# A hybrid encoder block on one core: the opening stage written in program order

## The chip, the cores and the metric

The kernel runs on one core of one Trainium2 chip. The core has TensorE (PE, matrix products; PEld is its weight load), VectorE (DVE), ScalarE (ACT), GpSimd (POOL) and SyncE (SP, which issues DMA transfers here). Each engine works through its own list of instructions in order, and waits where one needs a result of another engine. The metric is the device time of one execution in microseconds (us). Before the change: 984.22 us, the median of three runs (984.08 to 984.52).

## The reference

One layer of an encoder trunk on x of 512 positions by 1024 channels, float32. What matters for the opening:

```python
def rms_norm(x, g):
    xf = x.astype(jnp.float32)
    y = xf * lax.rsqrt(jnp.mean(xf * xf, axis=-1, keepdims=True) + EPS)
    return (y * g.astype(jnp.float32)).astype(x.dtype)
...
        hn = rms_norm(h, g_mix_pre[i])
        proj = hn @ w_in[i]
        z_sgu, z_conv, z_pool, z_gate = jnp.split(proj, SPLITS, axis=-1)
...
    a, gate = jnp.split(z, 2, axis=-1)
    h = a * jax.nn.sigmoid(gate)
```

Behind that come three token mixers (a spatial gating unit, a depthwise convolution of width 31, and multi-scale pooling), their merging by gates, an output product, a SwiGLU layer and a gated embedding. The change touches none of these.

## The kernel before

Channels lie on the 128 partitions, positions along the free axis. x is eight tiles of 128 channels by 512 positions (x_all), and k counts them. Every float32 operand of a product is split in two parts: a rounded high part made on ScalarE (a CAST, or an ACTIVATE where a gain is multiplied in) and the low remainder made on VectorE. A product is then three: high by high, high by low, low by high (mm3, L207).

The opening computes the first three pairs of convolution blocks before the norm of x is known. For that, x times the gain g_mix_pre is split into xg (split_scaled, L349), and the weight slice k of 768 columns (first_raw, loaded by L134) into first (split, L356). The slices 5 to 7 are loaded into the buffers named raw. For each k, 18 products go into six PSUM banks, ps_first (L414). The inverse norm comes out later as a factor: the squares of x are made on ScalarE and added up in x_sums, by GpSimd from the third on (L358). One product with a constant matrix makes the mean (ps_stat), and rsqrt makes x_inv in eight dependent steps on VectorE (inv_rms, in the loop over k at STAT_K = 4). Then each tile of x is multiplied by gain and x_inv (tile nrm), and split into hn. The products behind the opening, ps_ag, take hn and the weight blocks of in_w_mix: five more pairs, of 24 products for a block. A block is loaded into a raw buffer (three of them), and split into hi and lo.

What sets the order: the kernel is written against a framework that schedules instructions itself, from buffers and dependencies. Only inside a block `with order():` do the instructions issued through dve, act_e and pe keep the written order among themselves (InOrder, L55). The opening before stands outside such a block, so the scheduler is free there. The loads go through SyncE in the written order: x_all and the weight slice in turn for each k. A transfer waits in that queue until one of eight earlier ones has landed.

Of the kernel before, what the change touches and what calls it, by code (L numbers as in the profile page):

```python
# [12 lines left out]
AF = mybir.ActivationFunctionType  # L13
ALU = mybir.AluOpType
PSUM = bass.MemoryType.PSUM

P = 128
T = 512
H = 256
D = 1024  # L20
KT = D // P
# [16 lines left out]
N_VEC = len(VECS) * KT  # L38
# [5 lines left out]
N_WARM = 8  # L44
# [1 line left out]
TAPS = (4, 3, 5, 3, 5)  # L46
TAPS_U = 4

STAT_K, STAT_A, STAT_H, STAT_F = 4, 2, 7, 2
MIX_CUT = ((), (0,), (1, 2), (3, 4, 5, 6, 7))  # L50
PLE_CUT = (1, 2, 3, 4, 5, 6, 8)
PLE_SPLIT = 3
# [29 lines left out]
def hybrid_block(  # L82
# [7 lines left out]
    nc = tc.nc  # L90
    order = InOrder(tc)
    dve, act_e, pe = order.engine(nc.vector), order.engine(nc.scalar), order.engine(nc.tensor)
# [9 lines left out]
    def bank(name):  # L102
        return psum.tile([P, T], F32, tag="ps", name=name)

    def wide_tile(name):
        return wide.tile([P, KT, T], F32, tag="wide", name=name)

    def slot(tag, name, dt=F32R, shape=(2, T)):
        return act.tile([P, *shape], dt, tag=tag, name=name, bufs=6 if tag == "tm" else 8)

    def t2(name, n=T):
        return tmp.tile([P, n], F32, tag="t2", name=name)

    def row(name):
        return stat.tile([P, T], F32, tag="row", name=name)


    vec = const.tile([P, N_VEC + WIDTH * KT], F32, name="vec")
    x_all = wide_tile("x_all")
    first_all = wide.tile([P, KT * T], F32, tag="wide", name="first_all")  # L120
    first_raw = []

    def first_cuts(k):
        return ((0, 2 * P), (2 * P, N_FIRST)) if k == 0 else ((0, N_FIRST),)

    nc.scalar.dma_start(out=vec[:, :N_VEC], in_=vecs[:, :N_VEC])
    for k in range(KT):
        if k < 5:
            first_raw.append(first_all[:, k * N_FIRST:(k + 1) * N_FIRST])
        else:  # L130
            first_raw.append(stream.tile([P, D], F32, tag="raw", name="raw")[:, :N_FIRST])
        nc.sync.dma_start(out=x_all[:, k], in_=xT[:, k])
        for c0, c1 in first_cuts(k):
            nc.sync.dma_start(out=first_raw[k][:, c0:c1], in_=w_first[k][:, c0:c1])  # L134

    def col(name, k):
        i = VECS.index(name) * KT + k
        return vec[:, i:i + 1]
# [9 lines left out]
    warm_up = const.tile([P, T], BF16, name="warm_up")  # L148
    dve.memset(warm_up, 0.0)
    ps = psum.tile([P, T], F32, tag="pst", name="ps_warm", bufs=1)  # L150
    for _ in range(N_WARM):
        pe.matmul(ps, lhsT=warm_up[:, :P], rhs=warm_up, start=True, stop=True)
    ident = const.tile([P, P], F32, name="ident")
    make_identity(nc, ident)
    cnt_i = const.tile([P, WINDOWS[-1]], I32, name="cnt_i")
# [6 lines left out]
    def split(hi, lo, src):  # L162
        act_e.copy(hi, src)
        dve.tensor_tensor(out=lo, in0=src, in1=hi, op=ALU.subtract)

    def split_scaled(hi, lo, src, scale):

        act_e.activation(out=hi, in_=src, func=AF.Copy, scale=scale)
        dve.scalar_tensor_tensor(out=lo, in0=src, scalar=scale, in1=hi,
                                       op0=ALU.mult, op1=ALU.subtract)  # L170
# [34 lines left out]
    weights = Weights()  # L205
# [6 lines left out]
    def blk(w, k):  # L212
        return w[:, k * P:(k + 1) * P]
# [23 lines left out]
    def rsqrt(y, a, t):  # L237

        dve.tensor_scalar(out=y.bitcast(I32), in0=a.bitcast(I32), scalar1=-0.5,
                          scalar2=RSQRT_SEED, op0=ALU.mult, op1=ALU.add)  # L240
        dve.tensor_tensor(out=t, in0=y, in1=y, op=ALU.mult)
        dve.scalar_tensor_tensor(out=t, in0=t, scalar=-RSQRT_C2 * RSQRT_S, in1=a,
                                 op0=ALU.mult, op1=ALU.mult)
        dve.scalar_tensor_tensor(out=y, in0=t, scalar=RSQRT_C1 * RSQRT_S, in1=y,
                                 op0=ALU.add, op1=ALU.mult)
        dve.tensor_tensor(out=t, in0=y, in1=y, op=ALU.mult)
        dve.tensor_tensor(out=t, in0=t, in1=a, op=ALU.mult)
        dve.scalar_tensor_tensor(out=t, in0=t, scalar=-10.0 / 3.0 * RSQRT_S ** 2, in1=t,
                                 op0=ALU.add, op1=ALU.mult)
        dve.scalar_tensor_tensor(out=y, in0=t, scalar=5.0 * RSQRT_S ** 4, in1=y,  # L250
                                 op0=ALU.add, op1=ALU.mult)

    def channel_mean(sums):

        ps = psum.tile([P, T], F32, tag="pst", name="ps_stat", bufs=1)
        ps = ps[:, :sums.shape[1]]
        pe.matmul(ps, lhsT=mean_mat, rhs=sums, start=True, stop=True)
        return ps

    def inv_rms(sums, y):  # L260

        rsqrt(y, channel_mean(sums), t2("rs_t", sums.shape[1]))

    def square(src, name="sq"):
        sq = t2(name, src.shape[1])
        act_e.activation(out=sq, in_=src, func=AF.Square)
        return sq

    def add_square(sums, src, i, engine):

        if i == 0:
            act_e.activation(out=sums, in_=src, func=AF.Square)
        else:
            add_sq(sums, square(src), i, engine)

    def add_sq(sums, sq, i, engine):
        if i == 1:
            dve.scalar_tensor_tensor(out=sums, in0=sq, scalar=EPS * D / P, in1=sums,
                                     op0=ALU.add, op1=ALU.add)
        else:  # L280
            engine.tensor_tensor(out=sums, in0=sums, in1=sq, op=ALU.add)
# [63 lines left out]
    xg = [slot("br", f"xg{k}") for k in range(KT)]  # L345
    x_sums = row("x_sums")
    first = []
    for k in range(KT):
        split_scaled(xg[k][:, 0], xg[k][:, 1], x_all[:, k], col("g_mix_pre", k))  # L349
        if k < 7:  # L350
            pair = [slot("cv" if k < 4 else "tm", "first", shape=(D,)) for _ in range(2)]
        else:
            pair = [stream.tile([P, D], F32R, tag=t, name=t) for t in ("hi", "lo")]
        first.append([w[:, :N_FIRST] for w in pair])
        for c0, c1 in first_cuts(k):
            split(first[k][0][:, c0:c1], first[k][1][:, c0:c1], first_raw[k][:, c0:c1])  # L356
    for k in range(KT):
        add_square(x_sums, x_all[:, k], k, nc.gpsimd)  # L358
    weights.ahead(2)
    nc.sync.dma_start(out=vec[:, N_VEC:], in_=vecs[:, N_VEC:])  # L360


    h_conv = [slot("cv", f"h_conv{i}", F32) for i in range(4)]
# [29 lines left out]
    def glu(k, ps_a, ps_g, scale=None):  # L393
        sig = t2("sig")
        src = ps_g
        if scale is not None:
            dve.tensor_tensor(out=sig, in0=ps_g, in1=scale, op=ALU.mult)
            src = sig
        act_e.activation(out=sig, in_=src, func=AF.Sigmoid)
        if scale is not None:  # L400
            dve.tensor_tensor(out=sig, in0=sig, in1=scale, op=ALU.mult)
        dve.tensor_tensor(out=h_of(k), in0=ps_a, in1=sig, op=ALU.mult)
        queue_conv(k)

    hn = [slot("hn", f"hn{k}") for k in range(KT)]
    x_inv = row("x_inv")
    conv_sum = row("conv_sum")
    banks = [bank("ps_first") for _ in range(2 * N_RAW)]
    for k in range(KT):
        if k == STAT_K:  # L410
            inv_rms(x_sums, x_inv)
        for i, (w, a) in enumerate(((0, 0), (1, 0), (0, 1))):
            for j, ps in enumerate(banks):
                pe.matmul(ps, lhsT=blk(first[k][w], j), rhs=xg[k][:, a],  # L414
                                 start=k == 0 and i == 0, stop=k == KT - 1 and i == 2)
    for i in range(KT):
        t = t2("nrm")
        dve.scalar_tensor_tensor(out=t, in0=x_all[:, i], scalar=col("g_mix_pre", i),
                                       in1=x_inv, op0=ALU.mult, op1=ALU.mult)
        split(hn[i][:, 0], hn[i][:, 1], t)  # L420
    for k in range(N_RAW):
        glu(k, banks[2 * k], banks[2 * k + 1], x_inv)
    for k in range(N_RAW, KT):
        pair = []
        for _ in range(2):
            ps = bank("ps_ag")
# [119 lines left out]
    def branch_tile(acts, taps):  # L546
        ps = bank("ps_br")
        product(ps, weights.get(), acts)
        drain(taps)
        return ps  # L550

    for n in range(KT + SGU_LAG):
# [7 lines left out]
        else:  # L560
            i = n - SGU_LAG
            ps = branch_tile(sgu_T, TAPS[2])
# [49 lines left out]
    for n in range(KT + POOL_LAG):  # L612
# [39 lines left out]
    for n in range(KT):  # L652
        ps = branch_tile(conv_T, 0)
# [64 lines left out]
    with order():  # L718
# [25 lines left out]
        banks = [bank("ps_f") for _ in range(2 * N_PAIR)]  # L744
# [65 lines left out]
    for n in range(KT - 2):  # L810
        ps = bank("ps_fo")
# [25 lines left out]
    with order():  # L837
        ps = bank("ps_fo")
        halves = [bank("ps_fo") for _ in HALVES]
        ffn_out(ps, KT - 2, 0, weights.get(2))  # L840
        w = weights.get(1)
        for b, hs in zip(halves, HALVES):
            ffn_out(b, KT - 1, 0, w, hs)
        w = weights.get(1)
        ffn_out(ps, KT - 2, 1, w)
        weights.ahead(3)
        w = weights.get(2)
# [9 lines left out]
        c0, c1 = ffn_out_cuts[1]  # L857
# [10 lines left out]
        k = 0  # L868
# [9 lines left out]
        banks = [bank("ps_pg") for _ in range(N_LAST)]  # L878
# [82 lines left out]
```

## Time and profile before

| what | value |
|---|---|
| median of three runs | 984.22 us |
| the profiled execution | 983.63 us |
| its span, first to last instruction | 981.9 us |
| TensorE busy | 973.8 us (99%) |
| VectorE busy | 677.3 us (69%) |
| ScalarE busy | 346.1 us (35%) |
| GpSimd busy | 88.2 us (9%) |
| granted clock | 1.0 |

The time is some 1.7 us longer than the span, by what lies around the first and last instruction. The busy share of TensorE counts products as modelled; a product at half its clock also counts as busy. So the share says that TensorE seldom waits, and nothing of how fast its products follow each other. The granted clock is that of a limiter and reads 1.00 even where the products are at the lower of the two clock levels; that level shows in the distance of their starts.

### The profile page before, as it was taken

How to read it: one execution, taken by the hardware profiler on the slowest of the kernel's cores; microseconds unless marked ns; L12 is line 12 of the kernel's file. 1: busy time of each engine (PE TensorE's matmuls, PEld its weight loads, DVE VectorE, ACT ScalarE, POOL GpSimd, SP SyncE). 2: the span in 40 equal slices, each digit the busy share in tenths (PEclk: the TensorE clock that was granted, in tenths of full speed). 3: DMA queues.
4: the chain of work that ended last, by engine and by line, in shares of the span. 5: the costliest groups of instructions: out<-in, count | busy, mean ns of one | idle time of the engine just before them, and what ended most of it. 6: DMA issues, size and time to landing. Idle time of an engine off the chain costs nothing.

```text
span 981.9 us, 11718 instructions
## 1 busy us (share of the span) xinstructions
PE 973.8 (99%) x4682; PEld 819.2 (83%) x4682; DVE 677.3 (69%) x903; ACT 346.1 (35%) x483; POOL 88.2 (9%) x64
## 2 busy tenths in 40 slices
PE   9999999999999999999999999999999999999998
PEld 6788888788888878888888998888888888888897
DVE  7898789999988899957555787544444432223575
ACT  6422333332224332146435443323232322223442
POOL 4000004000013712160000010000000000000000
PEclk9999999999999999999999999999999999999999
DMA  6433331323322322332338112323322333334312
GB/s 233 137 108 107 109 106 65 107 69 104 107 81 81 101 103 86 105 110 68 126 96 272 62 38 74 104 90 104 98 96 93 98 91 104 92 92 139 109 43 86
DMA packets 30006, 100.53 MB, mean 102 GB/s; under 512 B 3456, under 2 KB 3968, under 8 KB 29952
## 3 DMA queue, kind: packets, MB, share of 16 engines
q1 hardware_dynamic: 29808, 99.75, 30.9%
q8 instruction: 36, 0.59, 0.2%
q14 instruction: 18, 0.15, 0.0%
q10 hardware_dynamic: 144, 0.04, 0.0%
HBM read 97.68 MB, written 2.10 MB: 102 GB/s over the span
## 4 chain that ended last, share of the span: by engine, by line
PE 88%; DVE 7%; issue 2%; DMA 1%; ACT 1%; SPq 0%; DVEq 0%; ACTq 0%
PE ps_f L69 25%; PE ps_br L69 13%; PE ps_fo L69 12%; PE ps_gate L69 12%; PE ps_ag L69 5%; PE ps_pg L69 5%; PE ps_o L69 5%; PE ps_z L69 4%; PE ps_nat L69 4%; DVE lo L69 2%; DVE acc L69 2%; PE ps_ple L69 1%; PE ps_pool L69 1%; DVE v_all L69 1%; DMA first_all<-in_w_first 1%
## 5 line engine op out<-in xcount | busy, mean ns | idle before, releaser
L69 ACT CAST hi<-raw 128x1024 fp32r<-128x1024 f32 (+3 forms) x158 | 162.5, 1030 | 456.3 <-PE ps_br L69 88.4
L69 DVE TENSOR_TENSOR lo<-raw,hi 128x1024 fp32r<-128x1024 f32 (+3 forms) x158 | 206.2, 1306 | 107.0 <-ACT hi L69 106.5
L69 DVE SCALAR_TENSOR_TENSOR acc<-h_conv,vec,acc 128x511 f32<-128x511 f32 (+14 forms) x240 | 183.3, 764 | 5.2
L69 PE MATMUL ps_f<-hg,hi 128*128 128x512 f32 (+1 forms) x624 | 184.5, 379 | 0.0
L69 PEld LDWEIGHTS ps_f<-hg,hi 128*128 128x128 f32 x624 | 115.1, 188 | 21.7
L69 PE MATMUL ps_gate<-hn,hi 128*128 128x512 f32 x384 | 119.6, 392 | 0.9 <-DVE gated L69 0.9
L69 PE MATMUL ps_f<-hg,lo 128*128 128x512 f32 (+1 forms) x312 | 118.0, 379 | 0.0
L69 PE MATMUL ps_fo<-f,hi 128*128 128x512 f32 (+1 forms) x396 | 111.0, 366 | 0.0
L69 PEld LDWEIGHTS ps_gate<-hn,hi 128*128 128x128 f32 x384 | 72.0, 188 | 17.1 <-DVE gated L69 1.3
L69 PEld LDWEIGHTS ps_fo<-f,hi 128*128 128x128 f32 x396 | 71.7, 189 | 12.2
L69 PE MATMUL ps_nat<-hi,hn 128*128 128x512 f32 x256 | 78.8, 390 | 0.0
L69 PE MATMUL ps_gate<-hn,lo 128*128 128x512 f32 x192 | 74.9, 390 | 0.0
L69 PE MATMUL ps_fo<-f,lo 128*128 128x512 f32 (+1 forms) x198 | 72.5, 366 | 0.0
L69 PEld LDWEIGHTS ps_f<-hg,lo 128*128 128x128 f32 x312 | 58.7, 188 | 11.0
L69 PEld LDWEIGHTS ps_nat<-hi,hn 128*128 128x128 f32 x256 | 48.1, 188 | 10.0
L69 DVE TENSOR_TENSOR f<-ps_f,h_inv 128x512 f32<-128x512 f32 x22 | 15.2, 690 | 56.5 <-PE ps_f L69 56.5
L69 PE MATMUL ps_nat<-lo,hn 128*128 128x512 f32 x128 | 49.9, 390 | 0.0
L69 PE MATMUL ps_ag<-hn,hi 128*128 128x512 f32 x160 | 49.6, 391 | 0.2 <-DVE sig L69 0.2
L69 PEld LDWEIGHTS ps_fo<-f,lo 128*128 128x128 f32 x198 | 37.4, 189 | 6.0
L69 PEld LDWEIGHTS ps_gate<-hn,lo 128*128 128x128 f32 x192 | 36.1, 188 | 7.5
L69 DVE TENSOR_TENSOR silu<-ps_f,h_inv 128x512 f32<-128x512 f32 x22 | 15.2, 690 | 36.0 <-PE ps_f L69 35.9
L69 PE MATMUL ps_br<-pool,hi 128*128 128x512 f32 x128 | 39.6, 389 | 0.0
(214 smaller groups left out, 1566.5 us busy)
## 6 DMA issues: line engine op xcount, KB each, us to landing
raw<-in_w_mix SPq DMA_DIRECT2D x90, 512.0 KB, 3.2
raw<-in_w_ffn_in SPq DMA_DIRECT2D x44, 512.0 KB, 3.3
raw<-in_w_ffn_out SPq DMA_DIRECT2D x16, 448.0 KB, 3.3
raw<-in_w_ffn_out SPq DMA_DIRECT2D x8, 512.0 KB, 3.5
raw<-in_w_ple_gate SPq DMA_DIRECT2D x8, 512.0 KB, 4.2
x_all<-in_xT SPq DMA_DIRECT2D x8, 256.0 KB, 6.4
h_all<-in_xT SPq DMA_DIRECT2D x4, 512.0 KB, 5.2
out_dram<-pg SPq DMA_DIRECT2D x7, 256.0 KB, 2.0
```

The source lines that it names most:

```text
L69: inst = op(*args, **kw)
```

## The change

The opening moves into a block that keeps the written order. Loads: after the first two slices, two tiles of x go ahead of each weight slice. The first part of slice 0 is cast on VectorE. The squares are added on VectorE, interleaved with slices 1 to 3. The mean product moves from slice 4 to slice 3 (STAT_K 3), rsqrt behind slice 4, and two tiles of hn are made behind each of slices 5, 6 and 7, two more at the end. One more warm-up product, half as wide, is added. Slice 0 is multiplied in two parts.

```diff
+X_SQUARED = (0, 2, 5, 8)
+X_AHEAD = (1, 2, 4, 6, 8, 8, 8, 8)
+STAT_K, STAT_A, STAT_H, STAT_F = 3, 2, 7, 2
...
-        nc.sync.dma_start(out=x_all[:, k], in_=xT[:, k])
+        while x_ahead < X_AHEAD[k]:
+            nc.sync.dma_start(out=x_all[:, x_ahead], in_=xT[:, x_ahead])
+            x_ahead += 1
...
-    for _ in range(N_WARM):
-        pe.matmul(ps, lhsT=warm_up[:, :P], rhs=warm_up, start=True, stop=True)
+    for n in N_WARM * (T,) + (H,):
+        pe.matmul(ps[:, :n], lhsT=warm_up[:, :P], rhs=warm_up[:, :n], start=True, stop=True)
...
-    for k in range(KT):
-        add_square(x_sums, x_all[:, k], k, nc.gpsimd)
-    weights.ahead(2)
-    nc.sync.dma_start(out=vec[:, N_VEC:], in_=vecs[:, N_VEC:])
+    def first_high(k):
+        act_e.activation(out=xg[k][:, 0], in_=x_all[:, k], func=AF.Copy, scale=col("g_mix_pre", k))
+        for i, (c0, c1) in enumerate(first_cuts(k)):
+            cast = dve.tensor_copy if k == i == 0 else act_e.copy
+            cast(first[k][0][:, c0:c1], first_raw[k][:, c0:c1])
+
+    def first_low(k):
+        for i, (c0, c1) in enumerate(first_cuts(k)):
+            cs = slice(c0, c1)
+            dve.tensor_tensor(out=first[k][1][:, cs], in0=first_raw[k][:, cs], in1=first[k][0][:, cs],
+                              op=ALU.subtract)
+            if i == 0:
+                dve.scalar_tensor_tensor(out=xg[k][:, 1], in0=x_all[:, k], scalar=col("g_mix_pre", k),
+                                         in1=xg[k][:, 0], op0=ALU.mult, op1=ALU.subtract)
...
+    def normed(i):
         t = t2("nrm")
         dve.scalar_tensor_tensor(out=t, in0=x_all[:, i], scalar=col("g_mix_pre", i),
+                                 in1=x_inv, op0=ALU.mult, op1=ALU.mult)
         split(hn[i][:, 0], hn[i][:, 1], t)
+
+    n_sq = 0
+    with order():
+        for k in range(KT):
+            first_high(k)
+            first_low(k)
+            if k < STAT_K + 1:
+                while n_sq < X_SQUARED[k]:
+                    add_square(x_sums, x_all[:, n_sq], n_sq, dve)
+                    n_sq += 1
+            if k == STAT_K:
+                ps_x = channel_mean(x_sums)
...
+            if k == STAT_K + 1:
+                rsqrt(x_inv, ps_x, t2("rs_t"))
+                nc.sync.dma_start(out=vec[:, N_VEC:], in_=vecs[:, N_VEC:])
+            if k > STAT_K + 1:
+                normed(2 * (k - STAT_K - 2))
+                normed(2 * (k - STAT_K - 2) + 1)
+            weights.ahead(max(0, k + 3 - KT))
+        for i in range(2 * (KT - STAT_K - 2), KT):
+            normed(i)
```

What this does to the lists of the engines is shown at three places. On VectorE before, from the last step of the inverse root on (L69 and L72 are the line of the wrapper through which these engines are called; the numbers tell buffers apart):

```order
L69 SCALAR_TENSOR_TENSOR x_inv_235<-rs_t_317,x_inv_235 128x512
L69 SCALAR_TENSOR_TENSOR nrm_398<-x_all_77,vec_76,x_inv_235 128x512
L69 SCALAR_TENSOR_TENSOR nrm_402<-x_all_77,vec_76,x_inv_235 128x512
L69 SCALAR_TENSOR_TENSOR nrm_406<-x_all_77,vec_76,x_inv_235 128x512
L69 SCALAR_TENSOR_TENSOR nrm_410<-x_all_77,vec_76,x_inv_235 128x512
L69 SCALAR_TENSOR_TENSOR nrm_414<-x_all_77,vec_76,x_inv_235 128x512
L69 SCALAR_TENSOR_TENSOR nrm_418<-x_all_77,vec_76,x_inv_235 128x512
L69 TENSOR_TENSOR hn0_227<-nrm_398,hn0_227 128x512
L69 TENSOR_TENSOR hn1_228<-nrm_402,hn1_228 128x512
L69 TENSOR_TENSOR hn2_229<-nrm_406,hn2_229 128x512
L69 TENSOR_TENSOR hn3_230<-nrm_410,hn3_230 128x512
```

And VectorE after the change, from the same step on (first_145 and first_146 are the high and low part of slice 5, first_147 and first_148 of slice 6, hi_383 and lo_384 of the first mix block):

```order
L72 SCALAR_TENSOR_TENSOR x_inv_167<-rs_t_311,x_inv_167 128x512
L72 TENSOR_TENSOR first_146<-raw_94,first_145 128x768
L72 SCALAR_TENSOR_TENSOR xg5_131<-x_all_77,vec_76,xg5_131 128x512
L72 SCALAR_TENSOR_TENSOR nrm_343<-x_all_77,vec_76,x_inv_167 128x512
L72 TENSOR_TENSOR hn0_159<-nrm_343,hn0_159 128x512
L72 SCALAR_TENSOR_TENSOR nrm_347<-x_all_77,vec_76,x_inv_167 128x512
L72 TENSOR_TENSOR hn1_160<-nrm_347,hn1_160 128x512
L72 TENSOR_TENSOR first_148<-raw_96,first_147 128x768
L72 SCALAR_TENSOR_TENSOR xg6_132<-x_all_77,vec_76,xg6_132 128x512
L72 SCALAR_TENSOR_TENSOR nrm_373<-x_all_77,vec_76,x_inv_167 128x512
L72 TENSOR_TENSOR hn2_161<-nrm_373,hn2_161 128x512
L72 SCALAR_TENSOR_TENSOR nrm_377<-x_all_77,vec_76,x_inv_167 128x512
```

The multiplies by x_inv no longer stand six in a row; each is followed at once by the subtraction that needs ScalarE's cast of it, and the work of slices 5 to 7 now stands behind x_inv.

On ScalarE after the change, from the first cast of an hn tile on (hi_149 is the high part of slice 7, hi_383 and hi_419 of the first two mix blocks):

```order
L72 CAST hn0_159<-nrm_343 128x512
L72 CAST hn1_160<-nrm_347 128x512
L72 ACTIVATE xg6_132<-x_all_77,vec_76 128x512
L72 CAST first_147<-raw_96 128x768
L72 CAST hn2_161<-nrm_373 128x512
L72 CAST hn3_162<-nrm_377 128x512
L72 CAST hi_383<-raw_381 128x1024
L72 ACTIVATE xg7_133<-x_all_77,vec_76 128x512
L72 CAST hi_149<-raw_98 128x768
L72 CAST hn4_163<-nrm_409 128x512
L72 CAST hn5_164<-nrm_413 128x512
L72 CAST hi_419<-raw_417 128x1024
```

The high parts of slices 6 and 7 and of the mix blocks stand behind casts of hn; before, all of them stood ahead of the first of these.

On TensorE after the change, from slice 6 of the opening on (xg_132 and xg_133 belong to slices 6 and 7, hn_159 to hn_162 are the first four tiles of hn, hi and lo the first mix block):

```order
L72 MATMUL ps_first<-xg_132,first 128x512 x18
L72 MATMUL ps_ag<-hn_159,hi 128x512 x2
L72 MATMUL ps_ag<-hn_159,lo 128x512
L72 MATMUL ps_ag<-hn_160,hi 128x512 x2
L72 MATMUL ps_ag<-hn_160,lo 128x512
L72 MATMUL ps_ag<-hn_161,hi 128x512 x2
L72 MATMUL ps_ag<-hn_161,lo 128x512
L72 MATMUL ps_ag<-hn_162,hi 128x512 x2
L72 MATMUL ps_ag<-hn_162,lo 128x512
L72 MATMUL ps_first<-xg_133,hi 128x512 x6
L72 MATMUL ps_first<-xg_133,lo 128x512 x6
L72 MATMUL ps_first<-xg_133,hi 128x512 x6
```

Twelve products of the first mix block have moved ahead of slice 7, and nine more (the tiles 4 to 6 of hn) follow it; before, slice 7 came first and the products of the second mix block were mixed among those of the first.

## Rows read from the trace of the kernel before

**Rows 1.** Page, part 1: busy time, share of the span and instructions, by engine.
```profile
PE 973.8 (99%) x4682; PEld 819.2 (83%) x4682; DVE 677.3 (69%) x903; ACT 346.1 (35%) x483; POOL 88.2 (9%) x64
```
**Rows 2.** Chain of waits in order of time: start us, us, what.
```profile
35.87 4.07 DVE nrm L69 x6
...
45.53 50.43 PE ps_ag L69 x221
```
**Rows 3.** Timeline of PE: start us, us, instruction xcount [idle before it <-releaser].
```profile
1.33 3.59 PE L69 MATMUL ps_warm<-warm_up 128*128 128x512 bf16 x8 [1.33 <-DVE warm_up L69]
5.49 19.01 PE L69 MATMUL ps_first<-xg,first 128*128 128x512 f32 x75 [0.57 <-ACT first L69]
24.33 1.02 PE L69 MATMUL ps_stat<-x_sums,mean_mat 128*128 128x512 f32 x2
...
36.77 1.52 PE L69 MATMUL ps_first<-xg,hi 128*128 128x512 f32 x6
38.13 1.52 PE L69 MATMUL ps_first<-xg,lo 128*128 128x512 f32 x6
...
45.53 0.74 PE L69 MATMUL ps_ag<-hn,hi 128*128 128x512 f32 x2 [0.19 <-DVE sig L69]
...
68.60 0.62 PE L69 MATMUL ps_ag<-hn,hi 128*128 128x512 f32 x2
```
**Rows 4.** Stretches: PE alone (clock, DMA share, GB/s last), then tile ps_ag alone.
```profile
5.40:9.10 3.70, 3.61 (x9) 1.00 0.96 352
...
40.80:68.50 27.70, 27.46 (x120) 22.41 (x121) 1.38 (x2) 1.18 (x2) 1.00 0.24 79
```
**Rows 5.** Timeline of POOL, the first of six adds.
```profile
10.04 1.60 POOL L281 TENSOR_TENSOR x_sums<-x_sums,sq 128x512 f32<-128x512 f32 x1 [8.69 <-ACT sq L69]
```
**Rows 6.** Timeline of DVE in the opening.
```profile
12.38 1.78 DVE L69 SCALAR_TENSOR_TENSOR xg<-x_all,vec,xg 128x512 fp32r<-128x512 f32 x1
...
22.30 0.74 DVE L69 SCALAR_TENSOR_TENSOR xg<-x_all,vec,xg 128x512 fp32r<-128x512 f32 x1
...
23.83 0.74 DVE L69 SCALAR_TENSOR_TENSOR xg<-x_all,vec,xg 128x512 fp32r<-128x512 f32 x1
...
28.79 1.23 DVE L69 TENSOR_TENSOR lo<-raw,hi 128x1024 fp32r<-128x1024 f32 x1 [0.77 <-ACT hi L69]
29.93 0.68 DVE L69 TENSOR_SCALAR x_inv<-ps_stat 128x512 int32<-128x512 int32 x1
30.72 0.69 DVE L69 TENSOR_TENSOR rs_t<-x_inv 128x512 f32<-128x512 f32 x1
31.45 0.69 DVE L69 SCALAR_TENSOR_TENSOR rs_t<-rs_t,ps_stat 128x512 f32<-128x512 f32 x1
...
39.86 3.09 DVE L69 TENSOR_TENSOR hn<-nrm,hn 128x512 fp32r<-128x512 f32 x5
```
**Rows 7.** Timeline of ACT in the opening.
```profile
18.07 0.73 ACT L69 ACTIVATE xg<-x_all,vec 128x512 fp32r<-128x512 f32 x1
18.69 0.62 ACT L69 ACTIVATE sq<-x_all 128x512 f32<-128x512 f32 x1
19.21 0.82 ACT L69 CAST hi<-raw 128x768 fp32r<-128x768 f32 x1
...
27.70 1.05 ACT L69 CAST hi<-raw 128x1024 fp32r<-128x1024 f32 x1 [0.95 <-DMA raw<-in_w_mix]
...
43.64 0.62 ACT L69 CAST hn<-nrm 128x512 fp32r<-128x512 f32 x1 [3.05 <-DVE nrm L69]
```
**Rows 8.** Timeline of SP's DMA queue: issues of transfers.
```profile
8.66 0.33 SPq L132 DMA_DIRECT2D x_all<-in_xT  x1
9.69 0.33 SPq L134 DMA_DIRECT2D raw<-in_w_first  x1
10.33 0.33 SPq L132 DMA_DIRECT2D x_all<-in_xT  x1
```
**Rows 9.** DMA issues from 0 to 40 us: xcount, KB each, median us to landing.
```profile
b_bc<-in_gb_v SPq DMA_DIRECT2D x1, 512.0 KB, 8.4
```

More of the change, by code (lines that the diff above doesn't have):

```diff
@@ L47 @@
 TAPS_U = 4
-STAT_K, STAT_A, STAT_H, STAT_F = 4, 2, 7, 2
+X_SQUARED = (0, 2, 5, 8)
+X_AHEAD = (1, 2, 4, 6, 8, 8, 8, 8)
+STAT_K, STAT_A, STAT_H, STAT_F = 3, 2, 7, 2
 MIX_CUT = ((), (0,), (1, 2), (3, 4, 5, 6, 7))
@@ L126, in hybrid_block @@
     nc.scalar.dma_start(out=vec[:, :N_VEC], in_=vecs[:, :N_VEC])
+    x_ahead = 0
     for k in range(KT):
@@ L348, in hybrid_block @@
     for k in range(KT):
-        split_scaled(xg[k][:, 0], xg[k][:, 1], x_all[:, k], col("g_mix_pre", k))
         if k < 7:
@@ L354, in hybrid_block @@
         first.append([w[:, :N_FIRST] for w in pair])
-        for c0, c1 in first_cuts(k):
-            split(first[k][0][:, c0:c1], first[k][1][:, c0:c1], first_raw[k][:, c0:c1])
-    for k in range(KT):
-        add_square(x_sums, x_all[:, k], k, nc.gpsimd)
-    weights.ahead(2)
-    nc.sync.dma_start(out=vec[:, N_VEC:], in_=vecs[:, N_VEC:])
+    def first_high(k):
[11 more added lines that the diff above has]
+                                         in1=xg[k][:, 0], op0=ALU.mult, op1=ALU.subtract)
     h_conv = [slot("cv", f"h_conv{i}", F32) for i in range(4)]
@@ L408, in hybrid_block @@
     banks = [bank("ps_first") for _ in range(2 * N_RAW)]
[L409 to L416, printed above, removed]
+    def normed(i):
         t = t2("nrm")
         dve.scalar_tensor_tensor(out=t, in0=x_all[:, i], scalar=col("g_mix_pre", i),
-                                       in1=x_inv, op0=ALU.mult, op1=ALU.mult)
+                                 in1=x_inv, op0=ALU.mult, op1=ALU.mult)
         split(hn[i][:, 0], hn[i][:, 1], t)
+    n_sq = 0
[9 more added lines that the diff above has]
+                ps_x = channel_mean(x_sums)
+            for c0, c1 in first_cuts(k):
+                for i, (w, a) in enumerate(((0, 0), (1, 0), (0, 1))):
+                    for j in range(c0 // P, c1 // P):
+                        pe.matmul(banks[j], lhsT=blk(first[k][w], j), rhs=xg[k][:, a],
+                                  start=k == 0 and i == 0, stop=k == KT - 1 and i == 2)
+            if k == STAT_K + 1:
[7 more added lines that the diff above has]
+            normed(i)
     for k in range(N_RAW):
```

## The prediction

> **What bounds the kernel now.** I read the page first: TensorE is busy for 99% of the span and every other engine for 69% or less [rows 1], so a microsecond counts only if TensorE waits or idles in it. The chain of waits came next. In the opening it does not run through TensorE: it goes through the step on VectorE that makes the normed x (tile nrm) and joins TensorE at 45.53 us, from where TensorE leads [rows 2]. Then TensorE's timeline: eight warm-up products, a wait of 0.57 us, and the 144 products of the opening, broken by the product for the mean square, ps_stat, at 24.33 us. The one later wait of the opening is 0.19 us, at 45.53 us [rows 3]. The opening's products follow each other at 1.36 us for six, 0.2267 us each [rows 3]. Nine of them fall into the 3.70 us from 5.40 to 9.10 us [rows 4], so the first ones run at the lower of the two clock levels (512 columns at 1.2 GHz are 0.427 us), after a warm-up that a pause followed. Later ones run at the upper level. So TensorE has little to win here: at most the 0.57, the 0.19 and some 2 us of the lower clock.
>
> **A ruler.** The five weight blocks behind the opening (ps_ag) hold 120 products. In the profile all 120 start before 68.50 us [rows 4] and the next starts at 68.60 us [rows 3]. Behind that point the order of the engines is the same in both kernels but for single rows, so I ask when the changed kernel gets there, and add the difference to the profiled execution's 983.63 us. That run is 0.59 us below the median of 984.22.
>
> **What leaves and comes, off the path.** The six adds on GpSimd go, and with them the slow VectorE steps: a step of 0.74 us takes 1.78 us beside an add on GpSimd [rows 5, 6]. Seven adds come to VectorE instead. The cast of the first weight columns moves to VectorE. Its price is not in the trace: a floor is nothing and a ceiling the 1.23 us of the widest subtraction there [rows 6], and either is over long before VectorE has to start on the third weight slice. The extra half-width warm-up product costs between nothing and a full warm-up product (8 take 3.59 us, [rows 3]). I take half of one, 0.2 us, so the first real product starts at about 4.9 us instead of 5.49. That gain is not kept, as the next part shows.
>
> **The chain that decides.** On VectorE the changed kernel runs everything in the written order, and each normed tile is now a round trip: multiply on VectorE, cast on ScalarE, subtract on VectorE, with nothing of VectorE's between. My prices:
> - weight subtraction plus low half of xg, 1.53 us (22.30 to 23.83) [rows 6]
> - a step that reads the one before it, 0.73 us (30.72 to 31.45); an independent one 0.60 us (five in 3.09) [rows 6]
> - a 1024-wide subtraction, 1.14 us (28.79 to 29.93) [rows 6]
> - on ScalarE a cast of a weight slice 0.82 us, a 512-wide step 0.52 us and an xg step 0.62 us to the next start, the hn cast itself 0.62, a 1024-wide cast 1.05 [rows 7]
> - a handover 0.04 us (28.75 to 28.79) [rows 6, 7]
>
> One normed tile is then 0.74 + 0.04 + 0.62 + 0.04 + 0.60 = 2.04 us. In the kernel before six multiplies ran ahead of the subtractions and the casts lay beside them.
>
> Third weight slice: SyncE issues each transfer when an earlier one has landed, so the issues at 8.66, 9.69 and 10.33 us date the landings: 1.03 us for a slice, 0.64 for a tile of x [rows 8]. The slice lands behind one more tile of x, at 9.69 + 0.64 = 10.33. Its cast ends at 11.15 and VectorE starts at 11.19. From there VectorE has three rounds of weight and xg work and six dependent adds: 3 x 1.53 + 6 x 0.73 = 8.97, to 20.16. The adds are over at 18.6, where ps_stat can start; its 1.02 us [rows 3] end before VectorE is ready, so this is no extra wait for VectorE. The inverse root is 8 x 0.73 = 5.84, to 26.00 (before: done as nrm starts, 35.87 [rows 2]). So x_inv is some 10 us earlier, and then:
> - slice 5: 1.53, to 27.53; two normed tiles, to 31.61
> - slice 6: ScalarE has its xg and its cast behind the second hn cast (at 30.35): 30.87, 31.49, end 32.31. VectorE waits 0.74, works 1.53, to 33.88
> - two normed tiles, to 37.96; the first mix block's cast (37.22 to 38.27), its subtraction 38.31 to 39.45
> - slice 7: xg 38.27, cast 38.89 to 39.71, VectorE 39.75 to 41.28; two normed tiles, to 45.36
> - second mix block: cast 44.62 to 45.67, subtraction to 46.85; seventh normed tile: subtraction starts at 48.29, ends 48.97.
>
> TensorE's row order is fixed too: slices 0 to 2, ps_stat, slices 3 to 6, twelve products of the first mix block, slice 7, nine more products of that block. It waits at ps_stat (from 17.2 at the earliest until 18.6), for slice 6 (until 32.3), for the first mix block (38.3 and 39.4) and for the low half of the seventh normed tile (49.0). At that last wait 19 of the 120 ps_ag products are done. The other 101 take 22.9 us, so the point that lay at 68.60 comes at 71.9: 3.3 us later.
>
> **Sum.** 983.63 + 3.3 = 986.9 us, 2.7 us over the median shown. What was the cover before and is gone: the scheduler had put products of the second mix block where the first waited for a normed tile, so that the wait was 0.19 us [rows 3]. Now that block stands behind all nine products. What is late next, if the chain were shorter, is TensorE itself.
>
> A rule against a term: the dependent steps stand 0.73 us apart, the independent ones 0.60 [rows 6]. The Trainium skill (VectorE: DVE Perf Modes, "The DRAIN you can't avoid") says that a semaphore behind each operation costs nothing extra. By it the 14 dependent steps would be 0.13 us shorter each, the chain 1.8 us, and the kernel at 985.1. The trace disagrees and decides for the root; the six adds on VectorE no row shows yet.
>
> **The rivals.**
> B, the products set the end (faster). If the casts do not hold VectorE up (eight normed tiles at 0.66 + 0.60 instead of 2.04 are 6.2 us less, which is more than TensorE's waits), TensorE runs from 4.9 us without one: 264 products at 0.2267 (59.85) and 1.02 for ps_stat, to 65.8. If the clock rises only at 9.1 as before, ten products pay 0.2 us more, 67.8. That is 980.8 to 982.8 us, middle 981.8. For it: so little idle time is in the kernel before, and x_inv really is ready 10 us sooner. Against it: the order on both engines is fixed, and in it no second multiply stands ahead of a subtraction. What the clock does matters for this rival alone. In mine TensorE arrives at ps_stat between 17.2 and 19.2 us, and VectorE is the later one either way.
> On that clock, the Trainium skill (TensorE: Matmul & The Clock Gate, "What's actually happening") says that the lower level is the default state and that activity lifts it. By it the closed pause would bring the rise forward, to the 980.8 end of B; no row here shows that.
> C, the chain is shorter by 0.7 to 3 us (no change). Its place is the 14 dependent steps, at 0.60 instead of 0.73: 1.8 us less, 985.1. For it: six of the 14 stand in no row. Against it: the same kinds of step in the root stand at 0.73. It decides from 0.7 us on, where the time falls under 986.2.
> D, slower still: on SyncE the two wide rows g_bc and b_bc now stand ahead of the second mix block and share the transfers with it. I put that block in at 44.6 us; it can be asked for at about 33.4, when slice 6 has left its buffer, and 8.4 us, what b_bc took from issue to landing [rows 9], leaves 2.8 us. If it lands more than that late, each further microsecond is one; two give 988.9.
>
> **How the numbers follow.** No change means within 0.2%, about what a measurement of this kernel can tell: 982.25 to 986.19 us. Chances: mine 0.70, C 0.15, B 0.09, D 0.06. My own range is 986.0 to 988.2: some 50 steps read to 0.01 or 0.02 us each, and 0.6 us more if the runs lie above the profiled one as before. With C and most of D it is 984.6 to 988.6; B stays out. Faster 0.09 (B); same 0.18 (C and the low edge of mine); slower 0.73.
>
> **What would show it.** Right: the first product at about 4.9 us and no pause behind the warm-up; VectorE's steps at 0.95 and 0.75 us throughout the opening, none at 1.8; a VectorE timeline in which each nrm is followed by an idle stretch of about 0.65 us up to its hn; x_inv near 26 us; waits of TensorE on ScalarE or VectorE at ps_stat, slice 6, the first mix block and the seventh normed tile, some 5 us together; the 121st ps_ag product near 71.9. Wrong, if TensorE is without waits between 20 and 50 us (then B), if the adds stand 0.6 us apart (C), or if a wait on the second mix block's transfer shows (D). If the waits are there and the time is not longer, then something behind the opening gave them back, and the ruler was wrong.

## The result, and the profile after the change

The changed kernel takes 988.33 us (median of six runs, 987.85 to 990.03) against 984.56 us of the kernel before (six runs, 984.08 to 986.05). The ratio is 1.0039, with a 95% interval of 1.0026 to 1.0052: slower by 3.8 us. The forecast was slower, at 986.9 us with a range of 984.6 to 988.6. The time lies in the range, 1.4 us above the forecast, and 0.1 us above the narrower range of 986.0 to 988.2 that the prediction gave for its own mechanism.

The profiled execution took 988.94 us (span 987.2 us). Its page shows TensorE as busy as before [rows 1]:

```profile
PE 975.8 (99%) x4683; PEld 819.2 (83%) x4683; DVE 677.8 (69%) x910; ACT 345.8 (35%) x482; POOL 78.9 (8%) x58
```

So the 5.3 us by which this execution is longer than the profiled one of before (988.94 less 983.63) can't be read there. They can be read in TensorE's timeline (start us, us, instruction, count, idle time before it and what ended it), which answers to [rows 3]:

```profile
1.33 3.81 PE L72 MATMUL ps_warm<-warm_up 128*128 128x512 bf16 x9 [1.33 <-DVE warm_up L72]
4.93 13.64 PE L72 MATMUL ps_first<-xg,first 128*128 128x512 f32 x54
20.13 1.10 PE L72 MATMUL ps_stat<-x_sums,mean_mat 128*128 128x512 f32 x2 [1.56 <-DVE x_sums L72]
20.66 17.23 PE L72 MATMUL ps_first<-xg,first 128*128 128x512 f32 x72
39.43 0.73 PE L72 MATMUL ps_ag<-hn,hi 128*128 128x512 f32 x2 [1.54 <-ACT hi L72]
40.69 0.80 PE L72 MATMUL ps_ag<-hn,lo 128*128 128x512 f32 x1 [0.52 <-DVE lo L72]
...
50.10 0.61 PE L72 MATMUL ps_ag<-hn,hi 128*128 128x512 f32 x2
50.56 0.39 PE L72 MATMUL ps_ag<-hn,lo 128*128 128x512 f32 x1
51.30 0.74 PE L72 MATMUL ps_ag<-hn,hi 128*128 128x512 f32 x2 [0.36 <-DVE sig L72]
...
73.88 0.62 PE L72 MATMUL ps_ag<-hn,hi 128*128 128x512 f32 x2
```

The first product is at 4.93 us without a pause (before: 5.49 behind a wait of 0.57), but four waits follow where the kernel before had one of 0.19: at the mean product, twice at the first mix block, and at 51.30 us. The 121st ps_ag product, the ruler of the forecast, starts at 73.88 instead of 68.60 us: 5.28 us later, and the execution is 5.31 us longer. The whole loss is made in the opening, and nothing behind it gives it back.

VectorE's timeline behind the inverse root shows why, beside [rows 6]:

```profile
26.50 0.69 DVE L72 SCALAR_TENSOR_TENSOR x_inv<-rs_t,x_inv 128x512 f32<-128x512 f32 x1
27.11 0.95 DVE L72 TENSOR_TENSOR first<-raw,first 128x768 fp32r<-128x768 f32 x1
...
28.64 0.74 DVE L72 SCALAR_TENSOR_TENSOR nrm<-x_all,vec,x_inv 128x512 f32<-128x512 f32 x1
30.07 0.69 DVE L72 TENSOR_TENSOR hn<-nrm,hn 128x512 fp32r<-128x512 f32 x1 [0.69 <-ACT hn L72]
30.68 0.74 DVE L72 SCALAR_TENSOR_TENSOR nrm<-x_all,vec,x_inv 128x512 f32<-128x512 f32 x1
32.11 0.69 DVE L72 TENSOR_TENSOR hn<-nrm,hn 128x512 fp32r<-128x512 f32 x1 [0.69 <-ACT hn L72]
...
49.30 0.69 DVE L72 TENSOR_TENSOR hn<-nrm,hn 128x512 fp32r<-128x512 f32 x1 [0.69 <-ACT hn L72]
49.90 0.74 DVE L72 SCALAR_TENSOR_TENSOR nrm<-x_all,vec,x_inv 128x512 f32<-128x512 f32 x1
50.57 1.88 DVE L72 TENSOR_TENSOR sig<-ps_first,x_inv 128x512 f32<-128x512 f32 x3
```

x_inv is ready at 27.1 us, 8.8 us earlier than before [rows 2]. But each normed tile is a round trip of 2.04 us (28.64 to 30.68) in which VectorE stands idle for 0.69 us until ScalarE has cast. The view of waits has seven such stretches, 4.8 us together:

```profile
DVE hn L72 <- ACT hn L72: 4.8, 7, 0.7
```

### The profile page after: what moved, and what is told of

Its sections match the earlier page's. It is cut to its first block, busy times and chain, and to the rows that moved or that the text cites. A ratio compares the mean times of both kernels' runs of the same rounds, so it can differ in the third digit from the quotient of the medians.

```text
span 987.2 us, 11711 instructions
## 1 busy us (share of the span) xinstructions
PE 975.8 (99%) x4683; PEld 819.2 (83%) x4683; DVE 677.8 (69%) x910; ACT 345.8 (35%) x482; POOL 78.9 (8%) x58
## 4 chain that ended last, share of the span: by engine, by line
PE 88%; DVE 8%; issue 2%; ACT 2%; DMA 1%; SPq 0%; DVEq 0%; ACTq 0%
PE ps_f L72 24%; PE ps_br L72 13%; PE ps_fo L72 12%; PE ps_gate L72 12%; PE ps_ag L72 5%; PE ps_pg L72 5%; PE ps_o L72 5%; PE ps_z L72 4%; PE ps_nat L72 4%; DVE lo L72 2%; DVE acc L72 2%; PE ps_ple L72 1%; PE ps_pool L72 1%; DVE v_all L72 1%; DMA first_all<-in_w_first 1%
## 5 line engine op out<-in xcount | busy, mean ns | idle before, releaser
L72 ACT CAST hi<-raw 128x1024 fp32r<-128x1024 f32 (+2 forms) x158 | 162.3, 1030 | 450.8 <-PE ps_br L72 88.4
L72 DVE TENSOR_TENSOR lo<-raw,hi 128x1024 fp32r<-128x1024 f32 (+2 forms) x158 | 207.2, 1312 | 104.6 <-ACT hi L72 103.8
L72 DVE SCALAR_TENSOR_TENSOR acc<-h_conv,vec,acc 128x511 f32<-128x511 f32 (+14 forms) x240 | 183.0, 763 | 5.2
L72 PE MATMUL ps_f<-hg,hi 128*128 128x512 f32 (+1 forms) x624 | 184.4, 378 | 0.0
L72 PEld LDWEIGHTS ps_f<-hg,hi 128*128 128x128 f32 x624 | 115.1, 188 | 21.8
L72 PE MATMUL ps_gate<-hn,hi 128*128 128x512 f32 x384 | 119.6, 392 | 0.9 <-DVE gated L72 0.9
L72 PE MATMUL ps_f<-hg,lo 128*128 128x512 f32 (+1 forms) x312 | 117.8, 378 | 0.0
L72 PE MATMUL ps_fo<-f,hi 128*128 128x512 f32 (+1 forms) x396 | 111.0, 366 | 0.0
L72 PEld LDWEIGHTS ps_gate<-hn,hi 128*128 128x128 f32 x384 | 71.9, 188 | 17.1 <-DVE gated L72 1.3
L72 PEld LDWEIGHTS ps_fo<-f,hi 128*128 128x128 f32 x396 | 71.7, 189 | 12.2
L72 PE MATMUL ps_nat<-hi,hn 128*128 128x512 f32 x256 | 78.8, 389 | 0.0
L72 PE MATMUL ps_gate<-hn,lo 128*128 128x512 f32 x192 | 74.8, 389 | 0.0
L72 PE MATMUL ps_fo<-f,lo 128*128 128x512 f32 (+1 forms) x198 | 72.4, 365 | 0.0
L72 PEld LDWEIGHTS ps_f<-hg,lo 128*128 128x128 f32 x312 | 58.7, 188 | 10.9
L72 PEld LDWEIGHTS ps_nat<-hi,hn 128*128 128x128 f32 x256 | 48.1, 188 | 10.0
L72 DVE TENSOR_TENSOR f<-ps_f,h_inv 128x512 f32<-128x512 f32 x22 | 15.1, 689 | 56.5 <-PE ps_f L72 56.5
L72 PE MATMUL ps_ag<-hn,hi 128*128 128x512 f32 x160 | 50.3, 397 | 1.9 <-ACT hi L72 1.5
L72 PE MATMUL ps_nat<-lo,hn 128*128 128x512 f32 x128 | 49.8, 389 | 0.0
L72 PEld LDWEIGHTS ps_gate<-hn,lo 128*128 128x128 f32 x192 | 36.0, 188 | 7.6
L72 PEld LDWEIGHTS ps_fo<-f,lo 128*128 128x128 f32 x198 | 37.3, 189 | 5.9
L72 DVE TENSOR_TENSOR silu<-ps_f,h_inv 128x512 f32<-128x512 f32 x22 | 15.2, 689 | 36.4 <-PE ps_f L72 36.3
L72 PE MATMUL ps_br<-pool,hi 128*128 128x512 f32 x128 | 39.6, 389 | 0.0
```

The costliest lines, as they stand in the source:

```text
L72: inst = op(*args, **kw)
```

## The experiments

My theory: the written order of VectorE and ScalarE behind x_inv sets the end (round trips, and the work of slices and mix blocks between them). The rivals: the load order, the squares on VectorE, the warm-up product and the clock. All variants were timed beside the kernel before, whose medians were 984.0 to 984.4 us.

**Pairs of round trips (e1).** Edit of the changed kernel:

```diff
-    def normed(i):
-        t = t2("nrm")
...
+    def normed(*tiles):
+        ts = [t2("nrm") for _ in tiles]
+        for i, t in zip(tiles, ts):
+            dve.scalar_tensor_tensor(out=t, in0=x_all[:, i], scalar=col("g_mix_pre", i),
+                                     in1=x_inv, op0=ALU.mult, op1=ALU.mult)
+        for i, t in zip(tiles, ts):
+            split(hn[i][:, 0], hn[i][:, 1], t)
...
-                normed(2 * (k - STAT_K - 2))
-                normed(2 * (k - STAT_K - 2) + 1)
+                normed(2 * (k - STAT_K - 2), 2 * (k - STAT_K - 2) + 1)
             weights.ahead(max(0, k + 3 - KT))
-        for i in range(2 * (KT - STAT_K - 2), KT):
-            normed(i)
+        normed(*range(2 * (KT - STAT_K - 2), KT))
```

> The changed kernel, but the normed tiles are made two at a time: both multiplies, then both casts and both subtractions, so that the cast of the first lies beside the second multiply. Theory (the written order of VectorE behind x_inv sets the end): a pair takes 2.7 instead of 4.1 us, the multiply of the gate tiles (sig) that frees the bank stands 3 to 4 us earlier, TensorE's waits on VectorE between 30 and 52 us shrink from some 3.0 to at most 1, and the 121st ps_ag product comes at 69 to 71 instead of 73.9: 984.5 us (983.5 to 985.5). Rival (the opening is late because its transfers or its mean product are late, and the round trips are hidden): x_inv is as late as before, so the time stays at 988.

Measured: 983.53 us, ratio to before 0.9996 (0.9987 to 1.0005). The loss is gone. VectorE, and the ruler on TensorE:

```profile
27.66 1.41 DVE L72 SCALAR_TENSOR_TENSOR nrm<-x_all,vec,x_inv 128x512 f32<-128x512 f32 x2
29.08 1.36 DVE L72 TENSOR_TENSOR hn<-nrm,hn 128x512 fp32r<-128x512 f32 x2
31.10 0.96 DVE L72 TENSOR_TENSOR first<-raw,first 128x768 fp32r<-128x768 f32 x1 [0.66 <-ACT first L72]
...
44.09 1.88 DVE L72 TENSOR_TENSOR sig<-ps_first,x_inv 128x512 f32<-128x512 f32 x3
```

```profile
19.15 1.10 PE L72 MATMUL ps_stat<-x_sums,mean_mat 128*128 128x512 f32 x2 [1.50 <-DVE x_sums L72]
...
68.16 0.62 PE L72 MATMUL ps_ag<-hn,hi 128*128 128x512 f32 x2
```

A pair takes 2.8 us (27.66 to 30.44) without an idle stretch instead of 4.2 (28.64 to 32.80 above), and TensorE waits no more behind the mean product. sig stands 6.5 us earlier, more than the 3 to 4 expected; 1.0 us of it lies ahead of the pairs, for in this execution the first nrm already came at 27.66 instead of 28.64. The 121st ps_ag product, at 68.16, came under the expected 69 to 71. Nothing ahead of x_inv was changed, so the rival falls.

**The scheduler free (e2).** All parts of the change stay; only the order is not kept:

```diff
-    with order():
+    with order(False):
         for k in range(KT):
```

> The changed kernel with all its parts (loads, squares on VectorE, warm-up product, slice 0 in two parts), but the opening is outside the block that keeps the written order, so that the scheduler orders it. Theory (the written order is the cause, the other parts cost nothing): six multiplies by x_inv stand in a row again, the 121st ps_ag product comes at 66 to 69 us, 981.5 to 984.5 us, no more than the kernel before. Rival (loads, squares or warm-up are the cause): over 986 us.

Measured: 981.99 us, ratio 0.9979 (0.9971 to 0.9988): the parts themselves are worth some 2 us, and their written order costs some 6.3 (988.33 less 981.99, from two sets of runs). VectorE's timeline in this version:

```profile
33.55 0.69 DVE L72 SCALAR_TENSOR_TENSOR x_inv<-rs_t,x_inv 128x512 f32<-128x512 f32 x1
34.28 4.07 DVE L72 SCALAR_TENSOR_TENSOR nrm<-x_all,vec,x_inv 128x512 f32<-128x512 f32 x6
38.26 3.09 DVE L72 TENSOR_TENSOR hn<-nrm,hn 128x512 fp32r<-128x512 f32 x5
```

Here x_inv is ready 7 us later than in the changed kernel, and the kernel is 6.3 us faster. Six multiplies in a row leave ScalarE time to cast beside them.

**Single parts undone: load order (e3) and squares (e4).**

```diff
-X_AHEAD = (1, 2, 4, 6, 8, 8, 8, 8)
+X_AHEAD = (1, 2, 3, 4, 5, 6, 7, 8)
```

> The changed kernel with the load order of the kernel before (x and weight slice in turn). Theory: the third slice lands 0.6 to 1.3 us earlier, but the last tile of x lands some 3 us later, at about 18, so the adds end where they did (about 19.8 to 20.5 us) and the time stays: 988.3 (987.3 to 989.3). Rival (the order of the loads costs the 3 us): 985 to 986.

Measured: 988.73 us, ratio 1.0051 (1.0037 to 1.0065), as expected: the load order isn't the cause.

```diff
-                    add_square(x_sums, x_all[:, n_sq], n_sq, dve)
+                    add_square(x_sums, x_all[:, n_sq], n_sq, nc.gpsimd)
```

> The changed kernel with the six adds of squares on GpSimd, as before. Theory (VectorE's adds are not dear by themselves): the adds on GpSimd take 1.5 us each and slow VectorE's steps beside them to 1.8 us; the mean product starts 1.5 to 3 us later than with VectorE's adds and everything behind x_inv with it: 990 us (989 to 991.5). Rival (seven more steps on VectorE cost the 3 us): 985 to 986.

Measured: 992.91 us, ratio 1.0095 (1.0082 to 1.0109): the sign was right, the size 1.4 us over the expected band. TensorE's timeline, and its clock (window, us, busy and count, granted clock, DMA share, GB/s):

```profile
22.78 2.08 PE L72 MATMUL ps_stat<-x_sums,mean_mat 128*128 128x512 f32 x2 [4.34 <-POOL x_sums L287]
```

```profile
22.80:25.00 2.20, 2.20 (x3) 0.50 0.00 0
25.00:30.00 5.00, 5.00 (x18) 0.74 0.02 3
```

The mean product is 2.65 us later than in the changed kernel, and behind the wait of 4.34 us TensorE ran at half its clock until 25 us and for part of the stretch up to 30, which I had not reckoned with. (The profiled run, 994.09 us, is the slowest of the four.) VectorE's adds are the better choice.

**The warm-up product: taken out (e5), and alone in the kernel before (e6).**

```diff
-    for n in N_WARM * (T,) + (H,):
+    for n in N_WARM * (T,):
```

> The changed kernel without the added half-width warm-up product. Theory: the pause before the first product opens again and more of the first products run at the lower clock level (up to 2 us later on TensorE), but all of it ends ahead of the wait at the mean product (1.56 us), which shrinks by as much: 988.3 us (987.5 to 989.0), the 121st ps_ag product at 73.3 to 74.3. Rival (the start of TensorE counts in this kernel): 989 to 990.

Measured: 990.03 us, ratio 1.0055 (1.0042 to 1.0068), outside my band and at the upper end of the rival's. Yet the start of TensorE wasn't what was lost: the pause did not open again (first product at 4.80 us, 13 products from 5.40 to 9.10 us), and the mean product came at 19.28, earlier than in the changed kernel. The number says nothing of the warm-up product, for the scheduler placed work from behind the ordered block in another way. VectorE in this version:

```profile
47.03 0.74 DVE L72 SCALAR_TENSOR_TENSOR nrm<-x_all,vec,x_inv 128x512 f32<-128x512 f32 x1
47.69 1.22 DVE L72 TENSOR_TENSOR lo<-raw,hi 128x1024 fp32r<-128x1024 f32 x1
48.83 0.68 DVE L72 TENSOR_TENSOR hn<-nrm,hn 128x512 fp32r<-128x512 f32 x1
```

A subtraction of the third mix block, 1.22 us, now stands ahead of the seventh tile's subtraction and of sig. TensorE waits there for the tile and for sig (0.6, 0.6 and 0.5 us in the view of waits), but it still starts the second block at 50.83, 0.5 us before the changed kernel. It falls behind after that: the 121st ps_ag product comes at 75.02, 1.1 us later than in the changed kernel, for the clock fell to its lower level (window, us, busy and count, granted clock, DMA share, GB/s):

```profile
51.40:54.70 3.30, 3.30 (x9) 0.50 0.08 30
```

That the other slow runs of this version lost their time in the same way is not shown. As a test of the warm-up product this run failed. The next one, an edit of the kernel before, does better:

```diff
-    for _ in range(N_WARM):
-        pe.matmul(ps, lhsT=warm_up[:, :P], rhs=warm_up, start=True, stop=True)
+    for n in N_WARM * (T,) + (H,):
+        pe.matmul(ps[:, :n], lhsT=warm_up[:, :P], rhs=warm_up[:, :n], start=True, stop=True)
```

> The kernel before with the half-width warm-up product alone. Theory (before, the chain over VectorE sets the start of the second mix block at 45.5 us): the first products go at the upper clock level, TensorE is some 1.5 us ahead by 40 us and then waits that much longer at 45.5: 984.0 us (983.5 to 984.5), with a wait of 1.5 to 2 us on VectorE. Rival (what the freely ordered version wins, 2 us, comes from the warm-up product and the clock alone): 982 to 982.5.

Measured: 984.46 us beside 984.44, ratio 1.0000 (0.9991 to 1.0009). What TensorE gains at the start it gives back further on. In the profile it is ahead by 0.5 us, not 1.5, at the last slice (36.25 against 36.77), and the view of waits has:

```profile
PE ps_ag L69 <- DVE hn L69: 2.0, 1, 2.0
...
PE ps_ag L69 <- DVE sig L69: 0.3, 1, 0.3
```

This execution is the slowest of the eleven (985.70 us), and VectorE's chain is 2.1 us later in it too (first nrm at 37.97 instead of 35.87), so the 2.0 us aren't all due to TensorE's earlier start.

**Squares on VectorE in the kernel before, alone (e9) and with the warm-up product (e10).**

```diff
-        add_square(x_sums, x_all[:, k], k, nc.gpsimd)
+        add_square(x_sums, x_all[:, k], k, dve)
```

> The kernel before with the six adds of squares on VectorE instead of GpSimd, nothing else. What the freely ordered version wins over the kernel before (2 us) can come from this (VectorE's steps of 1.8 us become 0.75, so the chain to the normed tiles is shorter) or from the warm-up product, or need both. Theory (both are needed: before, chain and products end within 0.2 us of each other at 45.5 us): TensorE's wait on VectorE at the normed tiles goes, its first products stay at the lower clock level, 983.8 us (983.2 to 984.3). Rival (the chain alone is the bound): 982.

> The kernel before with the six adds of squares on VectorE and the half-width warm-up product, in the old load order and with the scheduler free. Theory (these two parts together are what is good in the change): as the freely ordered version, 982.0 us (981.5 to 982.8), TensorE at the upper clock level from 7 us on and without a wait over 0.3 us behind it. Rival (the load order or the split of slice 0 is needed too): 983.5 or more.

Measured: 983.50 us alone, ratio 0.9988 (0.9979 to 0.9996); 982.01 us with the warm-up product (the edit of e6 too), 0.9982 (0.9973 to 0.9991). The second is the time of e2, so these two parts are enough for what is good in the change, and the load order and the split of slice 0 add nothing that shows. In the profiles the 121st ps_ag product comes at 68.60 us before, 68.47 in e9, and 66.97 in e10 and in e2. In e9 TensorE no longer waits at the normed tiles, and its start is left as the limit: 8 products from 5.40 to 9.10 us, 13 in e10. So by the profiles and the medians most of the gain needs both parts. The runs do not settle how much: the two intervals overlap, by the ratios the squares alone are worth 1.2 of 1.8 us, and four of the eleven runs of e9 (981.66 to 982.76) are about as fast as e10.

**The bank (e8).** In the changed kernel the last wait of TensorE is put down to sig, not to hn. The second ps_ag block takes a bank of ps_first, and the first multiply of sig frees it. The edit gives it the bank that ps_stat has left:

```diff
-            ps = bank("ps_ag")
+            if k == N_RAW and pair:
+                ps = psum.tile([P, T], F32, tag="pst", name="ps_ag", bufs=1)
+            else:
+                ps = bank("ps_ag")
```

> The changed kernel, but the second ps_ag block takes the bank that ps_warm and ps_stat have left instead of one of ps_first. Theory (the last wait is for a bank that sig frees, not for the seventh normed tile): the wait on sig goes, nothing else changes, the 121st ps_ag product comes 0.4 to 0.8 us earlier: 987.6 us (987.2 to 988.2). Rival (the seventh tile's low half is late anyway): a wait on hn in its place, 988.3 as before.

Measured: 987.36 us, ratio 1.0026 (1.0016 to 1.0037). The wait is gone and none comes in its place:

```profile
PE ps_ag L72 <- ACT hi L72: 1.6, 1, 1.6
...
PE ps_ag L72 <- DVE lo L72: 0.5, 1, 0.5
```

But more changed than the bank. With the bank free, TensorE's order changed too: two products stand at 47.62 us, ahead of ScalarE's cast of the seventh tile, so they can't be that tile's and must belong to the second block:

```profile
47.62 0.61 PE L72 MATMUL ps_ag<-hn,hi 128*128 128x512 f32 x2
```

```profile
47.73 0.62 ACT L72 CAST hn<-nrm 128x512 fp32r<-128x512 f32 x1 [1.96 <-DVE nrm L72]
```

So the rival's wait on the tile had no place to show, and this run does not tell the bank from the order that it allows. That the wait of the changed kernel was for the bank is read from its own rows: the first multiply of sig ends at 51.25 (50.57 and 0.68), and TensorE goes on at 51.30. The 121st product came 3.1 us earlier (70.74), not 0.4 to 0.8; but this execution is the fastest of its seven, its first nrm came 0.9 us earlier, and its clock did not fall, as the last section shows.

Against the changed kernel that is 1.0 us by the medians, 1.3 us by the ratios (0.0013 of 984), though the two were measured in different sets of runs and their intervals overlap.

**Another written order (e7).** Slices 0 to 7 first, the mean product one slice later, the inverse root behind slice 6, the normed tiles in two groups of four (with normed as in e1):

```diff
-            if k == STAT_K:
+            if k == STAT_K + 1:
                 ps_x = channel_mean(x_sums)
...
             if k == STAT_K + 1:
-                rsqrt(x_inv, ps_x, t2("rs_t"))
                 nc.sync.dma_start(out=vec[:, N_VEC:], in_=vecs[:, N_VEC:])
-            if k > STAT_K + 1:
-                normed(2 * (k - STAT_K - 2))
-                normed(2 * (k - STAT_K - 2) + 1)
-            weights.ahead(max(0, k + 3 - KT))
-        for i in range(2 * (KT - STAT_K - 2), KT):
-            normed(i)
+            if k == KT - 2:
+                rsqrt(x_inv, ps_x, t2("rs_t"))
+        normed(*range(KT // 2))
+        weights.ahead(1)
+        normed(*range(KT // 2, KT))
+        weights.ahead(2)
```

> The changed kernel in another written order: slices 0 to 7 first, the mean product one slice later on TensorE, the inverse root behind slice 6, then the normed tiles in two groups of four, the mix blocks' weights behind each group. x_inv is ready some 4 us later than in the changed kernel. Theory (what counts is that no round trip stands in VectorE's order and that nothing in TensorE's row order is late): TensorE has no wait over 0.3 us between 12 and 60 us, the 121st ps_ag product comes at 66 to 67.5, 981.0 to 982.8 us, some 2 us under the kernel before. Rival (a written order as such costs, or x_inv must be early): over 984.

Measured: 981.26 us (six runs, 980.85 to 982.06), ratio 0.9969 (0.9958 to 0.9981): the fastest version here, 3.2 us under the kernel before and 7 under the changed one. TensorE has a single wait of the opening, for the second slice's cast, and none behind it:

```profile
4.94 4.44 PE L72 MATMUL ps_first<-xg,first 128*128 128x512 f32 x18
10.22 12.57 PE L72 MATMUL ps_first<-xg,first 128*128 128x512 f32 x54 [0.84 <-ACT first L72]
22.62 1.02 PE L72 MATMUL ps_stat<-x_sums,mean_mat 128*128 128x512 f32 x2
...
67.02 0.62 PE L72 MATMUL ps_ag<-hn,hi 128*128 128x512 f32 x2
```

So a written order as such costs nothing; what stood in it did. Several things moved at once here, so the run does not say what each of them is worth.

## Why the prediction was right, and where its sum fell short

The verdict and its mechanism were right, and rivals B, C and D did not come. Step by step:

- First product: forecast about 4.9 us, measured 4.93. VectorE's slow steps of 1.78 us are gone. Both as said, and neither gain is kept.
- Third slice: I had it land at 10.33 and VectorE start on it at 11.19. VectorE started at 12.45 (the slice's subtraction in the first fence below), 1.26 us later. This step was mis-sized. The prices were right (0.67 us for a tile, 0.98 for a slice, by SyncE's issues at 9.87, 10.54 and 11.52), but the landing that they were counted from came later, and the slice landed at 11.52. ScalarE's rows show that it was late before the load orders differ: the second tile of x is waited for until 8.22 us (6.85 in the profile of before). But in e6, with the load order of before, it was 8.49, and in e1, with the new one, 7.26. It varies from one execution to the next, and I had read the date off one.

```profile
12.45 0.96 DVE L72 TENSOR_TENSOR first<-first_all,first 128x768 fp32r<-128x768 f32 x1 [0.17 <-ACT first L72]
13.32 0.74 DVE L72 SCALAR_TENSOR_TENSOR xg<-x_all,vec,xg 128x512 fp32r<-128x512 f32 x1
13.98 2.27 DVE L72 TENSOR_TENSOR x_sums<-x_sums,sq 128x512 f32<-128x512 f32 x3
16.18 0.95 DVE L72 TENSOR_TENSOR first<-first_all,first 128x768 fp32r<-128x768 f32 x1
```

```profile
8.22 0.72 ACT L72 ACTIVATE xg<-x_all,vec 128x512 fp32r<-128x512 f32 x1 [1.35 <-DMA x_all<-in_xT]
```

```profile
8.49 0.72 ACT L69 ACTIVATE xg<-x_all,vec 128x512 fp32r<-128x512 f32 x1 [1.44 <-DMA x_all<-in_xT]
```

```profile
7.26 0.73 ACT L72 ACTIVATE xg<-x_all,vec 128x512 fp32r<-128x512 f32 x1 [1.54 <-DMA x_all<-in_xT]
```

- Dependent adds, the point of rival C: three take 2.20 us (13.98 to 16.18), 0.73 each, as forecast, not 0.60. The Trainium skill (VectorE: DVE Perf Modes, "The DRAIN you can't avoid") found for eight copies that a semaphore behind each costs nothing extra. Carried over to adds that each read the one before, it would give 0.60, and the measurement decides.
- Round trips: 2.04 us forecast, 2.04 measured. From the end of the root (26.00 forecast, 27.11 measured) to the end of the seventh tile's low half (48.97, and 49.99 here) I had 22.97 us, and it took 22.88. The chain that decides is right to 0.1 us.
- Slice 6: I had TensorE wait until 32.3. It came at its work later itself and does not wait there. The other waits, 1.54 and 0.52 us at the first mix block, are where the forecast put them. The four waits make 4.0 us together, not some 5.
- The last wait: I put it at the seventh normed tile and had TensorE go on freely behind it. This step failed. From the tile's low half (ready at 49.99) TensorE would have been at the second block some 0.5 us later, at about 50.5; it started at 51.30, behind sig, which frees the bank. The pair behind the wait took 0.13 us longer too (51.30 to 51.88, where pairs take 0.45). That is 0.95 us. The term was missing, since I followed the tiles of the products and not their banks.
- The clock: after the waits at the mix block TensorE's products stood 0.43 us apart from 40.69 to 43.84 us. The granted clock there was 0.50, the lower level (1.2 GHz):

```profile
5.40:9.10 3.70, 3.70 (x15) 1.00 0.88 286
40.60:43.90 3.30, 3.21 (x8) 0.50 0.66 201
```

At the start the record read 1.00 although products stood 0.4 us apart [rows 4]; here it follows them. I had said that the clock matters for rival B alone. That was wrong as a rule, as e5 shows, but in this execution it cost nothing at the end: TensorE came to the second product of the seventh tile at 50.33, 0.3 us after its low half was ready, and then waited for sig, whose time is set by VectorE.

The sum: 71.9 forecast, 1.0 for the late slice and 0.95 for the bank make 73.85, against 73.88 measured. By the medians the miss is smaller, 1.4 us, since the other five runs lie 0.4 to 1.1 us under the profiled one, but for one at 990.03. That the slice came earlier in those is possible and not shown. So one term of the sum was too small and one was missing, both on the same side, and the time stayed in the range by 0.3 us, through the margin that was meant for rival D, which did not come. The verdict and the mechanism are earned; that the number held is partly luck.

## What to carry to other kernels

Making a value earlier is worth nothing if the order then puts a round trip between two engines behind each use: e2 has x_inv 7 us later than the changed kernel and is 6.3 us faster. When an order is written by hand, put all first halves of a handover ahead of the second halves, and follow for each product not only its inputs but the bank that it writes. Two parts that each shorten one of two equally late chains should be tried together: by the medians the two here gave 0.0 and 0.8 us alone and 2.2 together, though the runs leave open how much of that needs both.

## What the runs showed of the hardware that was not expected

After short waits TensorE's clock can fall to its lower level. In the changed kernel it read 0.50 from 40.6 to 43.9 us behind waits of 1.54 and 0.52 us, and in e5 from 51.4 to 54.7 behind three waits of 0.5 to 0.6; in e8, behind waits of 1.55 and 0.53 at the same place, it stayed at 1.00:

```profile
39.70:43.00 3.30, 3.23 (x14) 1.00 0.70 194
```

So it happens in some executions and not in others. In e8, where no bank wait hides it, the runs fall in two groups: 985.8 to 986.4 us (three, with a mean granted clock of 0.999 or 1.000) and 987.4 to 988.0 us (four, at 0.998). That the clock parts them is read from these means, for only the fastest run has a trace. What decides between the two I could not tell from these runs. That the clock can fall when TensorE pauses agrees with the Trainium skill (TensorE: Matmul & The Clock Gate, "What's actually happening"), for which the lower level is the default. At the start the rise did come forward as it would have it: 15 products in 5.40 to 9.10 us instead of 9 [rows 4]. Why it fell behind one pair of waits and not behind its like, no run here shows.
